# A decoder layer on one core: the end of its mixture-of-experts stage rewritten, and a four-expert pass moved to place 3

## The chip, the cores and the metric

The kernel runs on one core of a Trainium2 chip. The metric is the device time of one execution in microseconds (us). The time before is 546.1 us, the median of three runs (546.03 to 546.58).

## What is computed

One layer of a decoder with 512 tokens of width 1024, all float32: a projection, an mLSTM and a sliding-window attention, a first layer norm, then a hierarchical mixture of experts and a second layer norm. The change touches only the last part:

```python
x = layer_norm(ALPHA * x + y, ln1_w, ln1_b)
# router: top-1 group of 4, then top-2 of its 8 experts, weights in combine[token, expert]
for e in range(32):
    h = silu(x @ w_gate[e]) * (x @ w_up[e])          # 1024 -> 256
    out = out + combine[:, e:e+1] * (h @ w_down[e])  # 256 -> 1024
x = layer_norm(ALPHA * x + out, ln2_w, ln2_b)
```

Each expert has three matrices of 1 MB (gate, up, down), so 96 MB of weights are read once.

## The kernel before

**Passes.** The experts run in 13 passes of 128 seats each. ORDER names the kind of each pass: a B pass has two experts with 64 seats each, an A pass two with 96 and 32, a C pass four with 32 each. Before, ORDER is BBBABABACBBCC, with passes 0 to 12. A B or an A pass reads 6 MB, a C pass 12 MB. A pass takes these steps on TensorE: its tokens' rows are picked by one-hot matmuls (`pairs_x`, line 1005, for two passes at once, in odd passes, for the next two), gate and up (`pass_gu`, line 1092, in four parts; the transposes of the pass before stand ahead of the fourth), then, one pass later, the transposed product of the pass (`dn_t`, lines 1113 and 1115) and its down (`pass_dn`, line 1123).

**Combining.** The down results of passes 0 to 7 are scaled and written to DRAM (`y_store`, line 1141); in passes 8 and 9 `y_gather` fetches them token by token in eight indirect DMAs (line 1149), and VectorE adds them to x1 (line 1152). Later passes are split into a high and a low part (`y_split`, lines 1133 and 1134) and put back on their tokens by one-hot matmuls, with an add on VectorE for each half row (`add_back`, lines 1171 and 1172).

**Weights.** SyncE's queue issues every weight load, in the order of the passes, within a pass gate and up of k 0 to 511 of each expert, then of k 512 to 1023, then down. Each load of 1 MB takes one of 16 slots (`prefetch`, `load_part`); a slot is handed on in the order in which passes release gate and up, and a pass later down. So a load waits until an older pass has used its slot. I number the 96 slots' loads in order; the first 18 are passes 0 to 2.

**The end.** After pass 11 has run its gate and up in the loop, a block with a written order for TensorE, VectorE, ScalarE and GpSimd follows (line 1627 on): a first quarter of pass 12's gate and up (`last_gu`), pass 11's down, `add_back` by chunks of 128 tokens, and between them for each chunk `norm_s` (statistics on VectorE, then three small GpSimd instructions, lines 198, 199 and 1587), `norm_z` (ScalarE line 1595, multiply line 1596), the rest of pass 12's gate and up, `base_rows` (the rows of pass 12's tokens, for its own norm), pass 12's transposes and down, and `norm_o` (add, line 1601, and output DMA). At last pass 12's tokens are normed apart and scattered over the output (line 1697). On each engine the instructions of this block run in the order in which they are written. In the loop only TensorE's order is written.

Of the kernel before, what the change touches and what calls it, by code (L numbers as in the profile page):

```python
# [27 lines left out]
DE = 256  # L28
CAP = 64

ORDER = "BBBABABACBBCC"
NP = len(ORDER)
STATIC = 6
NOVER = 32
# [44 lines left out]
def layer_kernel(ctx, tc, x, w_in, conv_w, conv_b, gate_bias, norm_w, sinks, w_out, ln1_w, ln1_b,  # L79
# [30 lines left out]
    def rslot(name, dt=F32, n=DM):  # L110
        key = free.pop(0)
        return slot(name, dt, key)[:, :n], key
# [476 lines left out]
        return a.rearrange("(p j) n -> p j n", p=P)  # L589


    def load_part(ts, e, i):
        if i < 2:
            t = ts[0].rearrange("p (w j n) -> p w j n", w=2, j=4)
            for w, src in enumerate((w_gate[0], w_up[0])):
                SP.dma_start(t[:, w], rows_of(src, e)[:, 4 * i:4 * i + 4])
            return t
        src = rows_of(w_down[0], e)
        if len(ts) == 1:
            SP.dma_start(ts[0].rearrange("p (j n) -> p j n", j=2), src)  # L600
# [12 lines left out]
    def expert(r):  # L613
        if r < STATIC:
            return r
        if r not in ids:
            ids[r] = SP.value_load(eid[0:1, r:r + 1], min_val=0, max_val=NE - 1)
        return ids[r]

    def release(p, down):  # L620
        free.extend(k for k in KEYS[p][down] if k != "mix")

    def prefetch(n):
        while loads and free and n > 0:
            p, i, b = loads.pop(0)
            if free[0] == "mix":
                key, ts = free.pop(0), [slot("we")[:, :DM] for _ in range(2)]
            else:
                t, key = rslot("we", n=2 * DM)
                ts = [t]  # L630
            assert key != "mix" or i == 2
            KEYS[p][i == 2].append(key)
            pairs[p][b][i] = load_part(ts, expert(SEATS[p][b]), i)
            n -= 1


# [430 lines left out]
    def taken(p, t):  # L1067
        return pairs_g(t) if p in GATHER else pairs_x(t, min(2, NP - p))
# [93 lines left out]
    def toks(p):  # L1162
        return [t[:, p:p + 1] for t in tok2]
# [374 lines left out]

    def l2_fill(i):
        d, w = l2d  # L1540
        t = rslot("l2")[0]
        l2.append(t)
        for u in range(2):
            g = 2 * i + u
            p_ = bank("l2")
            for s in range(2):
                TE.matmul(p_, w[:, g:g + 1].to_broadcast([16, P]), d[:, s].rearrange("p k n -> p (k n)"),
                          start=s == 0, stop=s == 1)
            A.copy(t[:, 512 * u:512 * u + 512], p_)

    with tc.manual_schedule(engines={ENG.PE}):
        for p in range(2, NP - 1):
            release(p, False)
            if p > 2:
                release(p - 1, True)
            prefetch(99)
            hts = []
            pg = pg2 if p == 2 else pass_gu(xs, p % 2, p, (lambda: hts.append(dn_t(prev))) if prev else None)
            if prev:
                ht = hts[0]  # L1560
            h = pair_h(pg)
            if p % 2:
                xs = taken(p + 1, hn)
                if p + 3 < NP:
                    hn = ready(p + 3)
            if prev:
                py = pass_dn(ht, p - 1)
                if p - 1 < KEPT:
                    y_store(py, p - 1)
                else:  # L1570
                    y = y_split(py, cws[:, p - 1:p], *y_slots())
                    add_back(back_hot(slot("oh2", F32R)[:, 0:T], toks(p - 1)), y)
                if p - KEPT in (0, 1):
# [15 lines left out]
    zo = {}  # L1589

    def norm_z(c):
        z = zo[c] = rslot("z")[0]
        mv = mvs[c]
        for h, hs in enumerate(HS):
            A.activation(z[:, hs], x1[c][:, hs], AF.Identity, bias=mv[:, 3:4], scale=mv[:, 2:3])
            (G if ('VV', 'VG', 'VV', 'GV')[c][h] == "G" else V).tensor_mul(z[:, hs], z[:, hs], l2[0][:, hs])
# [11 lines left out]
    def same_rows():
        m, w = rslot("same")[0][:, 0:P], W.tile([P, DE], F32, name="hid", bufs=1)
        tk = tok2[0][:, p:p + 1]  # L1610
        b = bank("same", tag="t")
        TE.matmul(b[:, 0:P], tk.to_broadcast([P, P]), ident, start=True, stop=True)
        V.tensor_scalar(m, b[:, 0:P], tk, None, op0=OP.is_equal)
        V.scalar_tensor_tensor(w[:, 0:P], triu, 0.5, m, op0=OP.is_lt, op1=OP.mult)
        V.tensor_reduce(w[:, P:P + 1], w[:, 0:P], axis=AX.X, op=OP.add)
        V.tensor_scalar(w[:, P + 1:P + 2], tk, 0.0, None, op0=OP.is_lt)
        V.tensor_add(w[:, P:P + 1], w[:, P:P + 1], w[:, P + 1:P + 2])
        V.scalar_tensor_tensor(row[:, 0:1], w[:, P:P + 1], BIG, tk, op0=OP.mult, op1=OP.add)
        return m

    p = NP - 1
    release(p - 1, True)
    prefetch(99)
    l2d = l2_parts()
    o = back_hot(slot("oh2", F32R)[:, 0:T], toks(p - 1))
    with tc.manual_schedule(engines=MAN):
        ob = hots(p, P)
        pg = bank("pg")
        zr = [bank("zr", tag=t) for t in ("t", "m")]
        fin = {}  # L1630

# [12 lines left out]
        def last_gu(u, g):
            gu_part(pg, xs, 0, pairs[p], TILES[ORDER[p]], 2 * u + g)
            if g:
                k = len(SEATS[p])
                free.extend(KEYS[p][0][k * u:k * u + k])

        last_gu(0, 0)  # L1650
        ht = dn_t(prev)
        py = pass_dn(ht, p - 1)
        y = y_split(py, cws[:, p - 1:p], *y_slots())
        add_back(o, y, (0,))
        norm_s(0, base(0))
        l2_fill(0)
        add_back(o, y, (1,))
        l2_fill(1)
        norm_s(1, base(1))
        norm_z(0)  # L1660
        last_gu(0, 1)
        add_back(o, y, (2,))
        x1_fin(0)
        last_gu(1, 0)
        norm_s(2, base(2))
        sm = same_rows()
        add_back(o, y, (3,))
        base_rows(0)
        norm_z(1)
        base_rows(1)  # L1670
        last_gu(1, 1)
        norm_s(3, base(3))
# [12 lines left out]
        A.activation(held_y[:, HS[0]], py[0], AF.Copy, scale=cws[:, p:p + 1])
        A.activation(held_y[:, HS[1]], py[1], AF.Copy, scale=cws[:, p:p + 1])
        release(p, True)
        for h in range(2):
            TE.matmul(zr[h], sm, held_y[:, HS[h]], start=False, stop=True)
        norm_s(4, zr)  # L1690
        mv = mvs[4]
        z = rslot("z")[0]
        for h, hs in enumerate(HS):
            V.scalar_tensor_tensor(z[:, hs], zr[h], mv[:, 0:1], l2[0][:, hs], op0=OP.subtract, op1=OP.mult)
        for h, hs in enumerate(HS):
            V.scalar_tensor_tensor(z[:, hs], z[:, hs], mv[:, 2:3], l2[1][:, hs], op0=OP.mult, op1=OP.add)
        G.indirect_dma_start(out=o2[:, :], out_offset=bass.IndirectOffsetOnAxis(ap=row[:, 0:1], axis=0),  # L1697
                             in_=z, in_offset=None, bounds_check=T - 1, oob_is_err=False)
# [26 lines left out]
    free[:] = ["ring0"] * 4 + ["ring1"] * 2 + ["ring2"] + ["ring0", "ring1", "ring0", "ring2"]  # L1725
# [61 lines left out]
```

## Time and profile before

| what | value |
|---|---|
| median of the runs | 546.1 us |
| the profiled execution | 546.19 us, of which the span of instructions is 544.5 us |
| TensorE busy | 491.1 us (90%) |
| VectorE busy | 286.5 us (53%) |
| bytes read from DRAM | 126.58 MB |
| weights stream, main queue | 62.6% of 16 DMA engines' span |

Shares are averages over stages with different limits. The page also cuts the span into 40 slices of 13.6 us; in it TensorE is full from slice 21 to 28, the DMA engines are full from slice 20 to 36, and neither is full in the last three slices.

### The profile page before, as it was taken

Reading aid. Unit: us, or ns where it says so; the run is one execution under the profiler, and the core shown is the slowest. Engines: PE = TensorE matmul, PEld = TensorE weight load, DVE = VectorE, ACT = ScalarE, POOL = GpSimd, SP = SyncE. Lnnn points to the kernel's source line nnn. Section 1 sums busy time; section 2 is a strip of 40 time slices with the busy share of each in tenths; the row PEclk is TensorE's granted clock in tenths of the full one; section 3 lists DMA queues with packets and bytes.
Section 4 is the critical chain, followed back from the end, with each engine's and each line's share of the span. In section 5 each row is a group of like instructions: output and inputs, shape, how many; then the busy total and the mean of one; then the engine's idle time right before and its main releaser. Section 6 shows DMA issues by size and latency. Waiting matters only on the chain. (4 is left out here: it accounts for less than half of the span.)

```text
span 544.5 us, 8460 instructions
## 1 busy us (share of the span) xinstructions
PE 491.1 (90%) x3048; PEld 336.3 (62%) x3048; DVE 286.5 (53%) x643; ACT 162.6 (30%) x352; POOL 155.7 (29%) x179
## 2 busy tenths in 40 slices
PE   6999799999999999979899999999958687997990
PEld 5999688879889978768736463635413532362430
DVE  3453687874387675687881230210200564426883
ACT  3552555785543511505301112111110011020530
POOL 5479804322201103634900000000113031001451
PEclk9999979999999999987699999999987789998996
DMA  8624212221964637368379999999999999998003
GB/s 231 198 79 125 71 38 77 78 78 43 378 238 117 219 108 228 105 283 315 150 239 417 353 381 343 402 422 381 370 421 421 422 417 421 380 381 348 1 25 150
DMA packets 43885, 134.12 MB, mean 246 GB/s; under 512 B 6673, under 2 KB 17953, under 8 KB 40000
## 3 DMA queue, kind: packets, MB, share of 16 engines
q1 hardware_dynamic: 40928, 126.04, 62.6%
q0 software_dynamic: 2912, 7.50, 3.8%
q8 instruction: 25, 0.41, 0.3%
q14 instruction: 20, 0.16, 0.1%
HBM read 126.58 MB, written 8.91 MB: 249 GB/s over the span
## 5 line engine op out<-in xcount | busy, mean ns | idle before, releaser
L1092 PE MATMUL pg<-we,xs 128*32 128x512 f32 (+1 forms) x608 | 102.0, 606 | 8.7 <-DMA we<-in_w_exp_up 8.7
L1092 PEld LDWEIGHTS pg<-we,xs 128*32 128x32 f32 (+1 forms) x608 | 27.7, 121 | 67.6 <-issue 65.5
L1005 PE MATMUL xp<-ohr,x1h 128*128 128x256 f32 (+1 forms) x224 | 59.7, 304 | 7.1 <-DVE ht L1115 5.3
L244 PE MATMUL pj<-wh,xh 128*128 128x256 f32 (+1 forms) x224 | 63.7, 286 | 1.1 <-ACT wh L189 1.1
L245 PE MATMUL pj<-wh,xl 128*128 128x256 f32 (+1 forms) x224 | 62.8, 282 | 0.4 <-DVE xl L190 0.4
L1005 PE MATMUL xp<-ohr,x1l 128*128 128x256 f32 (+1 forms) x224 | 58.2, 297 | 0.0
L1123 PE MATMUL yo<-we,ht 128*32 128x512 f32 (+1 forms) x304 | 49.2, 620 | 6.5 <-DVE ht L1115 6.5
L1005 PEld LDWEIGHTS xp<-ohr,x1h 128*128 128x128 f32 x224 | 46.6, 208 | 12.9 <-DVE ht L1115 5.5
L249 PE MATMUL pj<-wl,xh 128*128 128x256 f32 x192 | 52.5, 279 | 0.0
L1005 PEld LDWEIGHTS xp<-ohr,x1l 128*128 128x128 f32 x224 | 46.5, 208 | 0.0
L244 PEld LDWEIGHTS pj<-wh,xh 128*128 128x128 f32 x224 | 42.4, 189 | 1.3 <-ACT wh L189 1.3
L245 PEld LDWEIGHTS pj<-wh,xl 128*128 128x128 f32 x224 | 42.4, 189 | 0.7 <-DVE xl L190 0.6
L1105 ACT ACTIVATE hid<-pg 128x256 f32<-128x256 f32 x13 | 5.0, 386 | 117.4 <-PE pg L1092 117.4
L1141 POOL DMA_DIRECT2D yd<-y x8 | 4.4, 552 | 124.5 <-ACT y L1140 124.5
L1123 PEld LDWEIGHTS yo<-we,ht 128*32 128x32 f32 (+1 forms) x304 | 14.5, 123 | 35.2 <-issue 25.4
L249 PEld LDWEIGHTS pj<-wl,xh 128*128 128x128 f32 x192 | 35.6, 188 | 0.0
L1115 DVE COPY ht<-ph 128x256 f32<-128x256 f32 x13 | 5.5, 422 | 55.3 <-PE ph L1113 55.3
L190 DVE TENSOR_TENSOR wl<-wraw,wh 128x1024 fp32r<-128x1024 f32 x14 | 21.4, 1543 | 22.8 <-ACT wh L189 19.1
L189 ACT ACTIVATE wh<-wraw 128x1024 fp32r<-128x1024 f32 (+2 forms) x23 | 23.2, 1023 | 12.4 <-DMA wraw<-in_w_in 3.7
L193 PE MATMUL pj<-xh,wh 128*128 128x512 f32 x64 | 26.5, 414 | 0.0
L195 PE MATMUL pj<-xl,wh 128*128 128x512 f32 x64 | 26.5, 414 | 0.0
L194 PE MATMUL pj<-xh,wl 128*128 128x512 f32 x64 | 26.1, 408 | 0.0
(359 smaller groups left out, 971.3 us busy)
## 6 DMA issues: line engine op xcount, KB each, us to landing
we<-in_w_exp_gate SPq DMA_DIRECT2D x64, 512.0 KB
we<-in_w_exp_up SPq DMA_DIRECT2D x64, 512.0 KB
we<-in_w_exp_down SPq DMA_DIRECT2D x30, 1024.0 KB
wraw<-in_w_in SPq DMA_DIRECT2D x20, 512.0 KB
yd<-y POOLq DMA_DIRECT2D x8, 512.0 KB, 7.7
xc<-in_x SPq DMA_DIRECT2D x4, 512.0 KB
wo<-in_w_out SPq DMA_DIRECT2D x8, 256.0 KB
wo<-in_w_out SPq DMA_DIRECT2D x4, 512.0 KB
```

Of the source, the lines that this page charges most:

```text
L189: A.activation(hi, src, AF.Copy)
L190: eng.tensor_tensor(lo, src, hi, op=OP.subtract)
L193: TE.matmul(o, lh, rh, start=start, stop=False)
L194: TE.matmul(o, ll, rh, start=False, stop=False)
L195: TE.matmul(o, lh, rl, start=False, stop=stop)
L244: TE.matmul(o, xh[j // 2][:, j % 2, cs], ws[i][j][0], start=j == 0, stop=False)
L245: TE.matmul(o, xl[j // 2][:, j % 2, cs], ws[i][j][0], start=False, stop=False)
L249: TE.matmul(o, xh[k // 2][:, k % 2, cs], ws[i][k][1], start=False, stop=k == 7)
L1005: TE.matmul(p_[:, j2, 0:P * n], w[c][:, 2 * g + j2], o[:, c, 0:P * n], start=c == 0 and s == 0 and j2 == 0, stop=c == NCH - 1 and s == 1 a ...
L1092: TE.matmul(pg[s:s + n], xs[k // 4][:, k % 4, P * b + s:P * b + s + n], ws[e][k // 4][:, :, k % 4], start=k == 0, stop=k == 7)
L1115: V.tensor_copy(ht, ph)
L1123: TE.matmul(py[u][s:s + n], ht[:, j, s:s + n], wt[e][2][j][:, 512 * u:512 * u + 512], start=j == 0, stop=j == 1)
```

## The change

ORDER becomes BBBCABABACBBC: one of the last two four-expert passes goes from place 11 to place 3, and the passes between move one place back. The down weights of pass 12 are loaded in two halves, first the half j=0 of its four experts, then the half j=1. In the last pass of the loop (p = 11) the transposes of pass 11 stand ahead of the `add_back` of pass 10. The one-hot rows of pass 12 (`ob`) are the tile made for its pick in the loop and are not built a second time, and `same_rows` moves into the loop's block. In the end block all of pass 12's gate and up stands behind pass 11's `add_back`, in two halves; its second half stands behind the norms of all four chunks. Some tiles come from the mix pool and no longer from the weights' slots. One of two scalings of pass 12's result moves from ScalarE to VectorE. The core of the diff:

```diff
-ORDER = "BBBABABACBBCC"
+ORDER = "BBBCABABACBBC"
...
+    loads.extend((NP - 1, 3, b) for b in range(len(SEATS[-1])))
...
+            last = p == NP - 1 and i == 2
+            if last:
+                late[b] = ts[0]
+            pairs[p][b][i] = load_part(ts, expert(SEATS[p][b]), i, 0 if last else None)
...
             if p % 2:
-                xs = taken(p + 1, hn)
+                ob, xs = hn, taken(p + 1, hn)
...
                     y = y_split(py, cws[:, p - 1:p], *y_slots())
+                    if p == NP - 2:
+                        ht = dn_t(h)
-                    add_back(back_hot(slot("oh2", F32R)[:, 0:T], toks(p - 1)), y)
+                    add_back(back(p - 1), y)
...
+        l2d = l2_parts()
+        o = back(NP - 2)
+        sm = same_rows(NP - 1)
...
-        ob = hots(p, P)
...
-        last_gu(0, 0)
-        ht = dn_t(prev)
-        py = pass_dn(ht, p - 1)
-        y = y_split(py, cws[:, p - 1:p], *y_slots())
+        y = y_split(pass_dn(ht, p - 1), cws[:, p - 1:p], *y_slots())
         add_back(o, y, (0,))
-        norm_s(0, base(0))
         l2_fill(0)
         add_back(o, y, (1,))
         l2_fill(1)
+        norm_s(0, base(0))
+        x1_fin(0)
+        add_back(o, y, (2,))
+        norm_z(0)
+        add_back(o, y, (3,))
+        pg = bank("pg")
+        last_gu(0)
         norm_s(1, base(1))
-        norm_z(0)
-        last_gu(0, 1)
-        add_back(o, y, (2,))
-        x1_fin(0)
-        last_gu(1, 0)
+        norm_o(0)
+        norm_z(1)
+        base_rows(0)
         norm_s(2, base(2))
-        sm = same_rows()
-        add_back(o, y, (3,))
-        base_rows(0)
-        norm_z(1)
         base_rows(1)
-        last_gu(1, 1)
+        norm_o(1)
+        norm_z(2)
+        base_rows(2)
         norm_s(3, base(3))
+        base_rows(3)
+        norm_o(2)
+        norm_z(3)
+        last_gu(1)
         h = pair_h(pg)
-        norm_z(2)
-        norm_z(3)
-        base_rows(2)
         ht = dn_t(h)
-        norm_o(0)
-        base_rows(3)
-        norm_o(1)
-        norm_o(2)
         norm_o(3)
         py = pass_dn(ht, p)
...
-        A.activation(held_y[:, HS[1]], py[1], AF.Copy, scale=cws[:, p:p + 1])
+        V.tensor_scalar(held_y[:, HS[1]], py[1], cws[:, p:p + 1], None, op0=OP.mult)
```

## Rows read from the trace of the kernel before

**Rows 1.** The page: DMA share and GB/s, 40 slices.
```profile
DMA  8624212221964637368379999999999999998003
GB/s 231 198 79 125 71 38 77 78 78 43 378 238 117 219 108 228 105 283 315 150 239 417 353 381 343 402 422 381 370 421 421 422 417 421 380 381 348 1 25 150
```

**Rows 2.** Timeline of SyncE's queue: start, duration; the last weight loads.
```profile
484.49 4.56 SPq L600 DMA_DIRECT2D we<-in_w_exp_down  x4
```

**Rows 3.** Timeline of TensorE, passes 8 and 9: start, duration, idle before.
```profile
393.78 1.88 PE L1092 MATMUL pg<-we,xs 128*32 128x512 f32 x10 [1.10 <-DMA we<-in_w_exp_up]
...
407.18 1.94 PE L1092 MATMUL pg<-we,xs 128*64 128x512 f32 x2 [5.81 <-DMA we<-in_w_exp_up]
...
418.82 1.94 PE L1092 MATMUL pg<-we,xs 128*64 128x512 f32 x8
...
428.14 0.58 PE L1005 MATMUL xp<-ohr,x1h 128*128 128x256 f32 x1 [5.31 <-DVE ht L1115]
```

**Rows 4.** Stretches: busy time by engine, then TensorE's clock, DMA share, GB/s.
```profile
312.00:316.00 4.00, 4.00 (x38) 1.25 (x34) 0.42 (x1) 0.00 (x0) 0.00 (x0) 1.00 0.92 295
...
328.00:332.00 4.00, 4.00 (x22) 1.41 (x20) 0.00 (x0) 1.13 (x2) 0.53 (x1) 1.00 0.74 247
332.00:336.00 4.00, 4.00 (x22) 1.14 (x22) 0.42 (x1) 0.00 (x0) 0.00 (x0) 1.00 1.01 343
```

**Rows 5.** Timelines of GpSimd and VectorE: the gathers of pass 8 and behind them.
```profile
410.73 1.12 POOL L1149 DMA_INDIRECT yg<-yd,yrow  x1 [5.89 <-issue]
...
426.53 1.23 DVE L1152 TENSOR_TENSOR x<-x,yg 128x1024 f32<-128x1024 f32 x1 [0.67 <-DMA yg<-yd,yrow]
427.67 0.42 DVE L1115 COPY ht<-ph 128x256 f32<-128x256 f32 x1
```

**Rows 6.** Timeline of TensorE, from pass 11's gate and up to its down.
```profile
468.83 5.36 PE L1092 MATMUL pg<-we,xs 128*32 128x512 f32 x48
...
487.29 1.05 PE L1092 MATMUL pg<-we,xs 128*32 128x512 f32 x4
...
494.78 1.90 PE L1092 MATMUL pg<-we,xs 128*32 128x512 f32 x10
...
499.87 5.34 PE L1123 MATMUL yo<-we,ht 128*32 128x512 f32 x32 [2.75 <-DVE ht L1115]
```

**Rows 7.** Timeline of VectorE, from pass 11's result to pass 12's down.
```profile
505.14 1.61 DVE L1134 SCALAR_TENSOR_TENSOR yl<-yo,cws,yh 128x512 fp32r<-128x512 f32 x2 [5.32 <-ACT yh L1133]
506.66 1.37 DVE L1172 TENSOR_TENSOR x<-x,cb 128x512 f32<-128x512 f32 x2
507.94 1.28 DVE L1583 BATCH_NORM_STATS2 lnst<-x 128x6 f32<-128x512 f32 x2
...
512.05 1.40 DVE L1596 TENSOR_TENSOR z<-z,l 128x512 f32<-128x512 f32 x2
...
525.76 0.41 DVE L1115 COPY ht<-ph 128x256 f32<-128x256 f32 x1
526.10 5.53 DVE L1601 TENSOR_TENSOR z<-z,l 128x512 f32<-128x512 f32 x6
```

**Rows 8.** Timeline of GpSimd: first and last small instruction of two chunks' norms.
```profile
509.56 0.24 POOL L198 TENSOR_SCALAR lnmv<-lnmv 128x1 f32<-128x1 f32 x1 [12.30 <-DVE lnmv L1585]
...
510.56 0.27 POOL L1587 TENSOR_SCALAR lnmv<-lnmv 128x1 f32<-128x1 f32 x1
512.14 0.69 POOL L198 TENSOR_SCALAR lnmv<-lnmv 128x1 f32<-128x1 f32 x1 [1.31 <-DVE lnmv L1585]
...
513.98 0.27 POOL L1587 TENSOR_SCALAR lnmv<-lnmv 128x1 f32<-128x1 f32 x1
```

**Rows 9.** Timeline of ScalarE: chunk 1's two halves in norm_z.
```profile
514.28 1.52 ACT L1595 ACTIVATE z<-x,lnmv 128x512 f32<-128x512 f32 x2 [0.61 <-POOL lnmv L1587]
```

**Rows 10.** Timeline of TensorE: the downs of passes 9 and 12.
```profile
458.35 3.65 PE L1123 MATMUL yo<-we,ht 128*64 128x512 f32 x16 [2.73 <-DVE ht L1115]
...
526.23 3.64 PE L1123 MATMUL yo<-we,ht 128*32 128x512 f32 x32 [1.02 <-DVE ht L1115]
```

More of the change, by code (lines that the diff above doesn't have):

```diff
@@ L589, in rows_of, with load_part @@
         return a.rearrange("(p j) n -> p j n", p=P)
-    def load_part(ts, e, i):
+    def load_part(ts, e, i, js=None):
         if i < 2:
@@ L599, in load_part @@
         if len(ts) == 1:
-            SP.dma_start(ts[0].rearrange("p (j n) -> p j n", j=2), src)
+            t = ts[0].rearrange("p (j n) -> p j n", j=2)
+            if js is None:
+                SP.dma_start(t, src)
+            else:
+                SP.dma_start(t[:, js], src[:, js])
             return [ts[0][:, 0:DM], ts[0][:, DM:2 * DM]]
@@ L621, in release @@
         free.extend(k for k in KEYS[p][down] if k != "mix")
+    loads.extend((NP - 1, 3, b) for b in range(len(SEATS[-1])))
+    late = {}
     def prefetch(n):
-        while loads and free and n > 0:
+        while loads and (free or loads[0][1] == 3) and n > 0:
             p, i, b = loads.pop(0)
+            if i == 3:
+                load_part([late[b]], expert(SEATS[p][b]), 2, 1)
+                continue
             if free[0] == "mix":
@@ L632, in prefetch @@
             KEYS[p][i == 2].append(key)
-            pairs[p][b][i] = load_part(ts, expert(SEATS[p][b]), i)
+            last = p == NP - 1 and i == 2
+            if last:
+                late[b] = ts[0]
+            pairs[p][b][i] = load_part(ts, expert(SEATS[p][b]), i, 0 if last else None)
             n -= 1
@@ L1540, in l2_fill @@
         d, w = l2d
-        t = rslot("l2")[0]
+        t = slot("l2")[:, :DM]
         l2.append(t)
@@ L1549, in l2_fill, with same_rows, back @@
             A.copy(t[:, 512 * u:512 * u + 512], p_)
+    def same_rows(p):
+        t = slot("same")
+        m, w = t[:, 0:P], t[:, P:2 * P + 2]
+        tk = tok2[0][:, p:p + 1]
+        b = bank("same", tag="t")
+        TE.matmul(b[:, 0:P], tk.to_broadcast([P, P]), ident, start=True, stop=True)
+        V.tensor_scalar(m, b[:, 0:P], tk, None, op0=OP.is_equal)
+        V.scalar_tensor_tensor(w[:, 0:P], triu, 0.5, m, op0=OP.is_lt, op1=OP.mult)
+        V.tensor_reduce(w[:, P:P + 1], w[:, 0:P], axis=AX.X, op=OP.add)
+        V.tensor_scalar(w[:, P + 1:P + 2], tk, 0.0, None, op0=OP.is_lt)
+        V.tensor_add(w[:, P:P + 1], w[:, P:P + 1], w[:, P + 1:P + 2])
+        V.scalar_tensor_tensor(row[:, 0:1], w[:, P:P + 1], BIG, tk, op0=OP.mult, op1=OP.add)
+        return m
+    def back(p):
+        return back_hot(slot("oh2", F32R)[:, 0:T], toks(p))
     with tc.manual_schedule(engines={ENG.PE}):
@@ L1558, in layer_kernel @@
             pg = pg2 if p == 2 else pass_gu(xs, p % 2, p, (lambda: hts.append(dn_t(prev))) if prev else None)
-            if prev:
-                ht = hts[0]
             h = pair_h(pg)
             if p % 2:
-                xs = taken(p + 1, hn)
+                ob, xs = hn, taken(p + 1, hn)
                 if p + 3 < NP:
@@ L1566, in layer_kernel @@
             if prev:
-                py = pass_dn(ht, p - 1)
+                py = pass_dn(hts[0], p - 1)
                 if p - 1 < KEPT:
@@ L1591, in norm_z @@
     def norm_z(c):
-        z = zo[c] = rslot("z")[0]
+        z = zo[c] = slot("z")[:, :DM]
         mv = mvs[c]
@@ L1605, in base @@
         return [x1[c][:, hs] for hs in HS]
[L1608 to L1619, printed above, removed]
     p = NP - 1
@@ L1623, in layer_kernel @@
     prefetch(99)
-    l2d = l2_parts()
-    o = back_hot(slot("oh2", F32R)[:, 0:T], toks(p - 1))
     with tc.manual_schedule(engines=MAN):
-        ob = hots(p, P)
-        pg = bank("pg")
         zr = [bank("zr", tag=t) for t in ("t", "m")]
@@ L1642, in base_rows, with last_gu @@
                     TE.matmul(zr[h], ob[:, c, 0:P].bitcast(F32), x1[c][:, HS[h]], start=c == 0, stop=False)
[L1644 to L1648, printed above, removed]
-        last_gu(0, 0)
-        ht = dn_t(prev)
-        py = pass_dn(ht, p - 1)
-        y = y_split(py, cws[:, p - 1:p], *y_slots())
+        def last_gu(u):
+            for g in range(2):
+                gu_part(pg, xs, 0, pairs[p], TILES[ORDER[p]], 2 * u + g)
+        y = y_split(pass_dn(ht, p - 1), cws[:, p - 1:p], *y_slots())
         add_back(o, y, (0,))
-        norm_s(0, base(0))
         l2_fill(0)
@@ L1658, in layer_kernel @@
         l2_fill(1)
-        norm_s(1, base(1))
-        norm_z(0)
-        last_gu(0, 1)
-        add_back(o, y, (2,))
-        x1_fin(0)
-        last_gu(1, 0)
+        norm_s(0, base(0))
[5 more added lines that the diff above has]
+        last_gu(0)
+        norm_s(1, base(1))
+        norm_o(0)
+        norm_z(1)
+        base_rows(0)
         norm_s(2, base(2))
-        sm = same_rows()
-        add_back(o, y, (3,))
-        base_rows(0)
-        norm_z(1)
         base_rows(1)
-        last_gu(1, 1)
+        norm_o(1)
+        norm_z(2)
+        base_rows(2)
         norm_s(3, base(3))
+        base_rows(3)
+        norm_o(2)
+        norm_z(3)
+        last_gu(1)
         h = pair_h(pg)
-        norm_z(2)
-        norm_z(3)
-        base_rows(2)
         ht = dn_t(h)
-        norm_o(0)
-        base_rows(3)
-        norm_o(1)
-        norm_o(2)
         norm_o(3)
         py = pass_dn(ht, p)
-        held_y = rslot("yf")[0]
+        held_y = slot("yf")[:, :DM]
         A.activation(held_y[:, HS[0]], py[0], AF.Copy, scale=cws[:, p:p + 1])
-        A.activation(held_y[:, HS[1]], py[1], AF.Copy, scale=cws[:, p:p + 1])
-        release(p, True)
+        V.tensor_scalar(held_y[:, HS[1]], py[1], cws[:, p:p + 1], None, op0=OP.mult)
         for h in range(2):
@@ L1691, in layer_kernel @@
         mv = mvs[4]
-        z = rslot("z")[0]
+        z = slot("z")[:, :DM]
         for h, hs in enumerate(HS):
@@ L1723, in dyn_pair @@
         add_back(back_hot(slot("oh2", F32R)[:, 0:T], [tk[:, i:i + 1] for i in range(2)]), y)
-    free[:] = ["ring0"] * 4 + ["ring1"] * 2 + ["ring2"] + ["ring0", "ring1", "ring0", "ring2"]
+    free[:] = ["ring0"] * 4 + ["ring1"] * 2 + ["ring2"]
     nmore = nc.values_load(more[0:1, 1:2], min_val=0, max_val=1)
```

## Prediction, made before the changed kernel was run

> **What bounds the kernel now.** I read the page's slices first, then the timelines backwards from the end. The slices show the weights streaming at about 420 GB/s until slice 36, then nothing [rows 1]. The last four downs are issued at 484.5 to 489 [rows 2] and slice 36 ends at 503.6, so every weight is in the chip by about 502; pass 12's down starts only at 526.23 [rows 10]. The last 42 us of the span are therefore not waiting for weights, and splitting the last down into halves can by itself save nothing: its cover is the 24 us between those two numbers, and it costs something only if the compute ahead of it came 24 us earlier.
>
> Going back from pass 12's down: its transposed tile is copied by VectorE at 525.76, and VectorE has been nearly full since pass 11's result came at 505.14 [rows 7]. Pass 11's down stood 2.75 us idle for VectorE, which was building one-hot rows, and then took 5.34 us [rows 6], where a down at full clock takes 3.65 [rows 10]. Before that, TensorE runs pass 11's gate and up from 468.83 [rows 6]. What sets 468.83 is further back: pass 9's gate and up waited 5.81 us for its first weights, and the pick behind it waited 5.31 us for VectorE [rows 3], which stood in its queue behind the adds of gathered rows [rows 5]. From there to 468.83 TensorE runs its passes one behind the other. So three points carry the end: when pass 9 is over, what lies between 468.83 (I call it S) and 505.14 (call it R, pass 11's result on VectorE), and VectorE's list from R to pass 12's down (D, 526.23).
>
> **Part 1: place 3, up to S.** Weights come in one order at one rate. Pass 9's gate and up is over when its last weights are in: before, that is load 64 (18 for passes 0 to 2, 30 for A B A B A, 12 for the C, 4 more); after, load 68, for pass 9 is then the C with eight gate and up loads. Load 61 landed at 407.18 [rows 3]. At 421 GB/s [rows 1] a load of 1.049 MB takes 2.49 us, so seven more take 17.4 us; a store and four gathers among them, some 1.3 MB, another 3.1 us: load 68 would land at 427.7 at the pace of before. The four-expert pass at place 3 has eight slots to release in one gate and up instead of four, so the stream doesn't thin where it does now: at 295, 247 and 343 GB/s for 4 us each against 421, that is 1.2 + 1.65 + 0.75 = 3.6 us [rows 4]. Load 68 then lands at 424.1, and the rest of the gate and up behind it (3 of 8 k steps at half clock, the transposes) ends near 428.6. Before, it ended at 420.76, but the pick had 1.9 us of work done and started again at 428.14 [rows 3], as if it had been free from 426.2. So S moves by 428.6 - 426.2 = **+2.4 us**.
>
> Bounds. If the stream gives back more than those three windows, pass 9 waits for nothing more than the gathers, and these come earlier by the 1.10 us and a like wait in pass 8's gate and up that go: -2.1. If pass 7 has to wait for weights too, later is the other end: load 56 landed at 393.78 [rows 3], load 52 four loads before it at the 2.68 us that lie between loads 56 and 61, less 3.6, at 379.5, while pass 7's gate and up would want it near 373. Then downs 6 and 7, the last store and the gathers behind it come 4.9 us later, and the copy at 427.67 that frees the pick stands behind them [rows 5]: +4.9. I take +2.4, because the landing at 407.18 is measured on the same stream and the gathers' place in VectorE's queue is not yet known. Passes 10 to 12 need fewer loads after that than before, and have them in time.
>
> **Part 2: from S to R.** Before, 36.3 us (468.83 to 505.14). Gone: the one-hot rows (2.75 us of idle TensorE), one quarter of gate and up ahead of the down (1.8), the slow down (5.34 - 3.65 = 1.7) [rows 6]. Transposes (0.5) move ahead into a gap. Added ahead of the down: the matmul of `same_rows` (0.5) and a copy of 0.4 in VectorE's queue; its five other instructions run under the down. Together -5.8. More is possible: the matmuls at 487.29 belong to the end block, yet run in the gaps of pass 10's `add_back` [rows 6]; if pass 11's down slips in likewise, VectorE's own list from 487.3 (split 1.5, one-hot rows 1.3, eight adds 5.1 [rows 7], copy 0.4, `same_rows` 1.3 and 0.3 more: 9.9 us) sets R at 497.2, which is -7.9. I take the middle, **-6.7**, since only part of a quarter slipped in before.
>
> **Part 3: from R to D.** Before, 21.1 us. VectorE runs this block in its written order. Its list before hid: split 1.61, four adds of 1.28, four statistics of 1.5, four multiplies by chunk (1.4 for two halves, 0.7 where GpSimd has one), `same_rows` 1.5, hid and the copy 0.4 each: about 19.6, and 1.5 us of waiting. After, `same_rows` is gone but `norm_o` of chunks 0, 1 and 2 (1.4, 1.4 and 0.7) moves from behind the copy [rows 7] to ahead of hid: 21.7 us of work and 0.6 of transposes. The new order puts only one short step (an add or an output add, 0.7 to 1.4 us) between a chunk's statistics and its multiply. Between them lie three GpSimd instructions, 1.27 us from first start to last end [rows 8], 0.1 of hand-over, and ScalarE's half, 0.76, the second half 0.76 later [rows 9]: 2.2 us to the first half and 3.0 to the second. VectorE then stands 1.0, 0.9, 0.9 and 2.3 us for chunks 0 to 3, and the last stands ahead of hid on ScalarE and on VectorE. With the first add's start this gives hid at R + 26.6 and D at R + 28.2: +7.1. In the second chunk the GpSimd steps took 2.11 us instead of 1.27 (512.14 to 514.25, the first one 0.69 instead of 0.24) while VectorE multiplied z by l [rows 7, 8]; after, output adds of that same kind run under two or more of the chunks' steps, 0.85 each: +8.8 or +9.1. I take **+8.8**. TensorE is done earlier (about R + 22.8: four adds' matmuls 5.7, two fills 2.4, gate and up 7.5, base rows 6.7), so VectorE decides.
>
> The Trainium skill ("SBUF — State Buffer", section "Who interferes with whom") says that a VectorE instruction with two SBUF inputs contends with a GpSimd instruction that reads SBUF and that the loser blocks entirely. The 0.69 and 2.11 us agree in direction; by the rule all four chunks would be hit when an output add starts first, which as an estimate would be a further 1.7 us and 553.6 in all; by the rows two are, and the sum goes by these.
>
> **Part 4: the clock.** TensorE waits 4 to 6 us for hid. After 2.73 us of waiting pass 9's down ran at full pace, 3.65 [rows 10]; after 2.75 pass 11's took 5.34 [rows 6]; after 5.31 the picks' first matmuls took 0.58 [rows 3]. The coming wait is nearest to the third: **+1.7**, bounds 0 and 2.1.
>
> **Part 5: from D to the end.** Before, 18.3 us. VectorE's six output adds (to 531.6, [rows 7]) no longer stand ahead of the last statistics, and one scaling is on an idle engine: **-0.5** (0.3 to 0.8). The three outputs leave earlier; only the fourth is near the scatter. The eight half loads are issued while the queue is full of loads, so they cost nothing that a later step sees.
>
> **Sum.** 2.4 - 6.7 + 8.8 + 1.7 - 0.5 = +5.7. The profiled execution took 546.19 us (span 544.5 and 1.7 around it), 0.1 above the median of its runs: 546.2 + 5.7 = 551.9 us.
>
> **Rivals.** (a) *The gathers late*: part 1 at +4.9 and part 3 at +9.1: 554.7 us. For it: the stream is full from slice 28 on [rows 1] and load 52 falls behind. Against: a wait of pass 7 also shortens later waits. (b) *The end is as long as it was*: the down slips into the gaps (-7.9), GpSimd isn't slowed (+7.1), half of the clock's loss (+0.8), S as before: 546.2 - 7.9 + 7.1 + 0.8 - 0.5 = 545.7, and up to 549 with S at +2.4. (c) *Faster*: the round over GpSimd and ScalarE costs VectorE no wait, because the steps of the next chunk cover it; then part 3 is only the work that moved, +1.2, TensorE doesn't idle and the clock holds: 546.2 + 2.4 - 6.7 + 1.2 - 0.5 = 542.6. It decides at the point where one intervening VectorE step is as long as 2.2 us; rows 7 show 1.4, which speaks against it; for it speaks that the three GpSimd steps alone, 1.27, are hidden by it. That the last down in halves is what counts can be left aside: it would need weights that are late, and they are 24 us early.
>
> **Chances.** The forecast (549 to 554) 0.45; (a) 0.13; (b) 0.18, of which 0.10 lies within 0.2% of the time before; (c) 0.24. A measurement of this kernel can tell about 0.2%, 1.1 us, from no change. Slower 0.45 + 0.13 + 0.08 = 0.66, same 0.10, faster 0.24. The range, 542.3 to 557, takes in (c), (a) and the upper bounds of the clock and of the slowed GpSimd; the forecast's own cases lie in 549 to 554.
>
> **What would show it.** Right: pass 9's gate and up waits 10 us or more for weights and S lies at 470 to 472; pass 11's down takes 3.65 us without a wait; VectorE idles ahead of line 1596's multiplies for ScalarE four times; TensorE idles some 4 us ahead of the last transposes; no weight lands after R. Wrong: S well before 468, R to D under 24 us, or weights that arrive after the last gate and up wants them, which would make the halves matter.

## The result, and the profile after

The changed kernel took 562.9 us (median of 4 runs, 558.6 to 566.5) against 546.1 us before: a ratio of 1.031, 95% interval 1.022 to 1.040. It is slower, as forecast, but by three times as much: 16.9 us and not 5.7. Its profiled execution took 565.51 us (span 563.8), 2.6 us above its median, so the sums below, made on profiles, come to +19.3 us of span and not to 16.9.

| stretch | before, us | after, us | change | forecast |
|---|---|---|---|---|
| start to pass 11's gate and up (S) | 468.8 | 481.6 | +12.8 | +2.4 |
| S to pass 11's result on VectorE (R) | 36.3 | 30.4 | -5.9 | -6.7 |
| R to pass 12's down (D) | 21.1 | 32.2 | +11.1 | +8.8 |
| D to the end | 18.3 | 19.5 | +1.2 | +1.7 - 0.5 |

The first row is counted from the start of the span. In the changed kernel's trace pass 0's gate and up starts at 268.29 and not at 269.78 (among all profiles here it lies between 265.8 and 269.8, whatever the edit), so counted from there S moved by 14.3 us.

The page of the changed kernel, its DMA share and GB/s in 40 slices of 14.1 us, is the answer to [rows 1]:

```profile
DMA  8644203214935562965599999999999999950110
GB/s 238 177 113 113 76 2 111 76 40 140 415 99 168 188 175 99 341 235 245 180 372 380 370 409 391 415 412 402 402 421 420 420 421 357 347 183 0 75 76 19
```

The stream thins less in slices 20 to 28 than it did, and it is over in slice 35, by 507.4 us; pass 12's down starts at 544.29. As before, the end doesn't wait for weights.

The loss ahead of S shows in TensorE's timeline (start, duration, idle before and what ended it): a wait of pass 7's gate and up, the last waits of pass 9's, the pick behind it, pass 9's down, and S. Line 1106 is line 1092 of before, 1019 is 1005, 1137 is 1123 and 1129 is 1115; it answers [rows 3] and the first of [rows 10]:

```profile
377.33 2.53 PE L1106 MATMUL pg<-we,xs 128*64 128x512 f32 x6 [2.58 <-DMA we<-in_w_exp_up]
...
418.76 1.02 PE L1106 MATMUL pg<-we,xs 128*32 128x512 f32 x2 [1.42 <-DMA we<-in_w_exp_up]
421.97 2.74 PE L1106 MATMUL pg<-we,xs 128*32 128x512 f32 x10 [2.19 <-DMA we<-in_w_exp_up]
...
425.27 2.38 PE L1106 MATMUL pg<-we,xs 128*32 128x512 f32 x16
427.58 0.38 PE L1019 MATMUL xp<-ohr,x1h 128*128 128x256 f32 x1
...
435.44 0.58 PE L1019 MATMUL xp<-ohr,x1h 128*128 128x256 f32 x1 [5.72 <-DVE ht L1129]
...
468.39 6.42 PE L1137 MATMUL yo<-we,ht 128*32 128x512 f32 x32 [6.85 <-DVE ht L1129]
...
481.64 2.80 PE L1106 MATMUL pg<-we,xs 128*64 128x512 f32 x12
```

The two copies (`ht`) that TensorE waits for stand in VectorE's queue behind adds of gathered rows. VectorE's timeline, the answer to [rows 5]:

```profile
423.86 1.23 DVE L1166 TENSOR_TENSOR x<-x,yg 128x1024 f32<-128x1024 f32 x1 [21.07 <-DMA yg<-yd,yrow]
...
430.61 1.23 DVE L1166 TENSOR_TENSOR x<-x,yg 128x1024 f32<-128x1024 f32 x1 [2.23 <-DMA yg<-yd,yrow]
433.83 1.23 DVE L1166 TENSOR_TENSOR x<-x,yg 128x1024 f32<-128x1024 f32 x1 [1.99 <-DMA yg<-yd,yrow]
434.97 0.42 DVE L1129 COPY ht<-ph 128x256 f32<-128x256 f32 x1
...
463.72 1.23 DVE L1166 TENSOR_TENSOR x<-x,yg 128x1024 f32<-128x1024 f32 x1 [6.60 <-DMA yg<-yd,yrow]
466.78 1.23 DVE L1166 TENSOR_TENSOR x<-x,yg 128x1024 f32<-128x1024 f32 x1 [1.83 <-DMA yg<-yd,yrow]
467.92 0.42 DVE L1129 COPY ht<-ph 128x256 f32<-128x256 f32 x1
```

So the last weights of pass 9 were in and its matmuls done at 427.6; the pick then ran 16 matmuls and stopped for a copy of pass 8's product, which stood behind the fourth add. GpSimd's timeline has the last store and the gathers that follow it. The last of the first four gathers was issued at 419.51 and added 14.3 us later:

```profile
406.50 0.53 POOL L1155 DMA_DIRECT2D yd<-y  x1 [8.61 <-DMA we<-in_w_exp_up]
...
415.47 1.12 POOL L1163 DMA_INDIRECT yg<-yd,yrow  x1 [6.59 <-issue]
...
419.51 0.99 POOL L1163 DMA_INDIRECT yg<-yd,yrow  x1 [0.30 <-issue]
```

In the kernel before, the same two instructions stand as follows, and the add of [rows 5] came 11.8 us behind the second:

```profile
402.45 0.53 POOL L1141 DMA_DIRECT2D yd<-y  x1 [10.74 <-ACT y L1140]
...
414.77 0.99 POOL L1149 DMA_INDIRECT yg<-yd,yrow  x1 [0.30 <-issue]
```

From R on, VectorE's timeline answers to [rows 7] (line 1631 is 1596, 1630 is 1595, 1636 is 1601):

```profile
516.70 0.69 DVE L1186 TENSOR_TENSOR x<-x,cb 128x512 f32<-128x512 f32 x1 [1.70 <-PE cb L1185]
...
520.71 0.69 DVE L1186 TENSOR_TENSOR x<-x,cb 128x512 f32<-128x512 f32 x1 [1.03 <-PE cb L1185]
...
522.17 2.54 DVE L1631 TENSOR_TENSOR z<-z,l 128x512 f32<-128x512 f32 x2
...
530.17 0.69 DVE L1631 TENSOR_TENSOR z<-z,l 128x512 f32<-128x512 f32 x1 [1.68 <-ACT z L1630]
...
535.20 1.40 DVE L1631 TENSOR_TENSOR z<-z,l 128x512 f32<-128x512 f32 x2 [1.67 <-ACT z L1630]
...
541.28 1.40 DVE L1631 TENSOR_TENSOR z<-z,l 128x512 f32<-128x512 f32 x1 [2.68 <-ACT z L1630]
```

TensorE waits at the end of it for the last product (`hid`) and then runs the down slowly, at a granted clock of 0.50 from 544 to 548:

```profile
543.07 0.70 PE L1127 MATMUL ph<-ident,hid 128*128 128x128 f32 x2 [5.26 <-DVE hid L1120]
544.29 6.02 PE L1137 MATMUL yo<-we,ht 128*32 128x512 f32 x32 [0.52 <-DVE ht L1129]
```

### The profile page after: what moved, and what is told of

It is laid out like the page before. It is cut to its first block, busy times and chain, and to the rows that moved or that the text cites. A ratio compares the mean times of both kernels' runs of the same rounds, so it can differ in the third digit from the quotient of the medians.

```text
span 563.8 us, 8436 instructions
## 1 busy us (share of the span) xinstructions
PE 501.7 (89%) x3048; PEld 337.6 (60%) x3048; DVE 282.8 (50%) x635; ACT 162.2 (29%) x351; POOL 154.8 (27%) x179
## 5 line engine op out<-in xcount | busy, mean ns | idle before, releaser
L1106 PE MATMUL pg<-we,xs 128*32 128x512 f32 (+1 forms) x608 | 105.5, 611 | 11.5 <-DMA we<-in_w_exp_up 11.4
L1019 PE MATMUL xp<-ohr,x1h 128*128 128x256 f32 (+1 forms) x224 | 58.4, 299 | 7.5 <-DVE ht L1129 5.7
L1137 PE MATMUL yo<-we,ht 128*32 128x512 f32 (+1 forms) x304 | 54.1, 671 | 8.0 <-DVE ht L1129 8.0
L1019 PE MATMUL xp<-ohr,x1l 128*128 128x256 f32 (+1 forms) x224 | 56.9, 293 | 0.0
L1166 DVE TENSOR_TENSOR x<-x,yg 128x1024 f32<-128x1024 f32 x8 | 9.8, 1224 | 35.8 <-DMA yg<-yd,yrow 35.8
```

Of the source, the lines that this page charges most:

```text
L1019: TE.matmul(p_[:, j2, 0:P * n], w[c][:, 2 * g + j2], o[:, c, 0:P * n], start=c == 0 and s == 0 and j2 == 0, stop=c == NCH - 1 and s == 1 a ...
L1106: TE.matmul(pg[s:s + n], xs[k // 4][:, k % 4, P * b + s:P * b + s + n], ws[e][k // 4][:, :, k % 4], start=k == 0, stop=k == 7)
L1137: TE.matmul(py[u][s:s + n], ht[:, j, s:s + n], wt[e][2][j][:, 512 * u:512 * u + 512], start=j == 0, stop=j == 1)
L1166: V.tensor_add(x1[c], x1[c], t)
```

## The experiments

Kernels that were sent together ran on one chip and share its runs of the kernel before (medians 546.3, 544.7 and 544.3 us in three groups). The ratio on record, with its interval, isn't always the quotient of the two medians (e2: 1.011 against 1.007); where they differ I name both. Then come the landmarks of each profiled execution, in us, "to R" counted from the first matmul of pass 0's gate and up. One execution is profiled of each kernel, and executions differ by some us:

| kernel | median us | ratio to before (95%) | to R | R to D | D to end |
|---|---|---|---|---|---|
| before | 546.1 | | 235.4 | 21.1 | 18.3 |
| after | 562.9 | 1.031 (1.022 to 1.040) | 243.8 | 32.2 | 19.5 |
| e1, order alone | 556.7 | 1.023 (1.013 to 1.033) | 241.7 | 21.3 | 19.4 |
| e2, end alone | 550.3 | 1.011 (1.006 to 1.015) | 228.8 | 33.1 | 18.5 |
| e3, after, gather adds on GpSimd | 550.9 | 1.008 (1.004 to 1.013) | 232.4 | 31.6 | 18.6 |
| e4, before, gather adds on GpSimd | 537.9 | 0.989 (0.979 to 0.999) | 225.3 | 23.1 | 18.2 |
| e5, after, end block interleaved as before | 558.1 | 1.028 (1.021 to 1.034) | 241.4 | 27.1 | 18.6 |
| e6, e5 with old order and gather adds on GpSimd | 531.6 | 0.976 (0.968 to 0.984) | 222.0 | 27.1 | 18.7 |
| e7, e5 with gather adds on GpSimd | 542.4 | 0.994 (0.989 to 1.000) | 228.6 | 27.0 | 18.6 |
| e8, after, each `norm_z` a chunk later | 557.6 | | 241.5 | 27.7 | 17.0 |
| e9, e6 with a quarter of gate and up in the gap | 533.2 | 0.980 (0.974 to 0.986) | 218.3 | 22.7 | 19.5 |
| e10, after, last down in one piece | 560.6 | 1.028 (1.023 to 1.034) | 239.2 | 33.2 | 18.3 |

**Which half of the change loses.** e1 is the kernel before with the new order only, e2 the changed kernel with the old order.

```diff
-ORDER = "BBBABABACBBCC"
+ORDER = "BBBCABABACBBC"
```

> The kernel before with only the order of the changed one (the four-expert pass at place 3); the end block stays as it was. Theory A (place 3 moves the start S of pass 11's gate and up by +12.8 us, because pass 8's and 9's transposed copies stand behind the gathers' adds in VectorE's queue and the gathers come later): S near 481, and 546.1 + 12.8 = 559 us, the stretches from S to R, from R to D and from D on as in the kernel before (36.3, 21.1, 18.3). Theory B (the late S comes out of the rewritten end's other use of buffers, and place 3 costs the +2.4 us of the forecast): 548.5 us.

```diff
-ORDER = "BBBCABABACBBC"
+ORDER = "BBBABABACBBCC"
```

> The changed kernel with the old order of passes. If the end is what it was in the changed kernel (S to R 30.4, R to D 32.2, D to the end 19.5 us) and S is back at 468.8, the sum is 546.1 - 5.9 + 11.1 + 1.2 = 552.5 us. Rival: the long stretch from R to D in the changed kernel came from the late S and the slow clock behind it, and the rewritten end saves what its shorter S to R says: 540 to 546 us.

e1 measured 556.7 us, 10.3 above before on its chip (2.3% by the ratio, some 12); e2 550.3, 4.0 above (1.1%, some 6), which is not the 540 to 546 of its rival. Both halves lose, and their sum, 14.3 by the medians and some 18 by the ratios, lies about the 16.9 of the whole. The order's loss lies ahead of R (R to D is 21.3, as before), the end's behind it: up to R the new end is 6.5 us faster than before, and from R to D 12.0 slower. The profile of e1 is of the fastest of its runs (550.7), with S at 471.8 where theory A had 481; in it the pick waited only 0.5 us and the down behind it 5.2. So its landmark of 241.7 understates the median's.

**The adds of gathered rows.** In the changed kernel (e3) and in the one before (e4) these adds go to GpSimd, which issues the gathers, and so out of VectorE's queue.

```diff
-                V.tensor_add(x1[c], x1[c], t)
+                G.tensor_add(x1[c], x1[c], t)
```

> The changed kernel with the eight adds of gathered rows (line 1166) on GpSimd instead of VectorE. Theory A (these adds hold the copies that free TensorE): the waits of 5.72 us in the pick and 6.85 us ahead of pass 9's down go, and so does the slow clock in that down (2.8), S comes near 468, 549 to 552 us. Rival (weights are next: passes 9 to 11 wait for their loads anyway): S stays above 477, at most 4 us gained, 559 us or more.

> The kernel before with the same eight adds on GpSimd. Theory A: the waits of 5.31 and 2.73 us go, 538 us. Rival (pass 10 or 11 then waits for weights, or add_back waits for GpSimd's slower adds): 543 to 547 us.

e3 measured 550.9, e4 537.9 us, both as theory A had it. In e3's timeline of TensorE the pick and pass 9's down start without a wait:

```profile
429.81 0.39 PE L1019 MATMUL xp<-ohr,x1h 128*128 128x256 f32 x1
...
457.28 3.64 PE L1137 MATMUL yo<-we,ht 128*32 128x512 f32 x32
```

and the gathers come hardly earlier, as its timeline of GpSimd has it:

```profile
434.76 2.41 POOL L1166 TENSOR_TENSOR x<-x,yg 128x1024 f32<-128x1024 f32 x1 [1.33 <-DMA yg<-yd,yrow]
```

The fourth add starts 0.9 us later than in the changed kernel (counted from pass 0's gate and up, 0.5 us earlier) and takes twice as long, and no copy stands behind it. So the two waits, 5.72 and 6.85 us, were an effect of the queue.

The move has a price of its own. While GpSimd adds, VectorE's one-hot steps take longer: two of them 4.59 us, where two like ones took 0.61 in the changed kernel, and one 2.49 instead of 0.34. Behind the latter TensorE's `add_back` waited 2.42 us. From e3's timeline of VectorE:

```profile
434.52 4.59 DVE L1012 TENSOR_SCALAR ohr<-iot,pcol 128x256 fp32r<-128x256 f32 x2
...
462.55 2.49 DVE L1173 TENSOR_SCALAR oh<-iot,tok 128x256 fp32r<-128x256 f32 x1
```

And e4 shows that the kernel before paid for the like waits: it gains 8.5 us of median by the same edit (by the ratio 1.1%, some 6, and hardly clear of nothing), the changed kernel about 12 (562.9 to 550.9, though these two ran on different chips). The waits alone are therefore only some 4 to 6 us of what the change added, and place 3 must cost more by itself.

**What place 3 costs without the gather waits.** e6 and e7 have the adds on GpSimd and an end block interleaved as before (e5's); they differ in ORDER alone.

> The kernel before with three things: gathers' adds on GpSimd, and from the change the early down of pass 11 with reused one-hot rows (S to R) and its other edits, with the old interleave behind it; old order of passes. If the parts add: 537.9 (adds on GpSimd) - 7 (S to R 30.4 instead of 37.4) = 531 us. Rival: with TensorE this early the last passes wait for weights (the stream ends near 500 in every run), and the parts don't add: 535 us or more.

> As the run with the old order, new front and GpSimd adds, but with the four-expert pass at place 3. Theory A: without the gathers' adds in the way, place 3 costs what four more loads ahead of pass 9's end cost: S some 3 us behind the kernel before and 10 to 14 behind the same kernel with the old order, 541 to 544 us. Rival: place 3 costs nothing any more and both orders give the same time within 2 us.

e6 measured 531.6 us, e7 542.4, in runs of one chip, as their theories had it (531; 541 to 544): place 3 costs 10.8 us with no gather in VectorE's way. TensorE's groups from pass 0's gate and up to R (line, shapes, count | busy us, mean ns | idle before, and for what) show where. e6:

```profile
L1106 PE MATMUL pg<-we,xs 128*64 128x512 f32 x224 | 55.5, 628 | 7.8 <-DMA we<-in_w_exp_up 7.8
...
L1106 PE MATMUL pg<-we,xs 128*32 128x512 f32 x320 | 37.4, 595 | 0.1
```

e7:

```profile
L1106 PE MATMUL pg<-we,xs 128*64 128x512 f32 x224 | 54.7, 611 | 2.6 <-DMA we<-in_w_exp_up 2.5
L1106 PE MATMUL pg<-we,xs 128*32 128x512 f32 x320 | 45.0, 628 | 9.3 <-DMA we<-in_w_exp_up 9.3
```

The same number of matmuls, busy and waiting together: 100.8 us in e6, 111.6 in e7. Of these 10.8 us, 4.0 are waits for weights (now in the four-expert pass, which takes its loads one by one), and 6.8 are busy time, in the short pieces between those waits: in e7 two matmuls by themselves are busy 1.02 us at 403.22, where 48 in one piece are 5.33, and the granted clock falls to 0.50 in the last stretch of waits (420 to 424). All that while the stream runs at 418 to 425 GB/s, so TensorE goes at its pace. Four more loads ahead of pass 9's end at 2.49 us each are, as an estimate, 10.0 us; no run tests that reading by itself. For the changed kernel and e2 the same rows give 109.0 and 100.4, +8.6; TensorE's waits for `ht` are 13.1 against 8.2, +4.9; and the downs are 1.4 longer: together 14.9, the whole difference of their R (243.8 - 228.8 = 15.0).

```profile
L1106 PE MATMUL pg<-we,xs 128*64 128x512 f32 x224 | 54.5, 608 | 3.7 <-DMA we<-in_w_exp_up 3.7
L1106 PE MATMUL pg<-we,xs 128*32 128x512 f32 x320 | 42.9, 604 | 7.9 <-DMA we<-in_w_exp_up 7.7
...
L1137 PE MATMUL yo<-we,ht 128*32 128x512 f32 x160 | 21.0, 671 | 6.8 <-DVE ht L1129 6.8
```

These are the changed kernel's. (The two profiles e6 and e7 differ by 6.5 in R and not by 10.8, since e6's is of its slowest run, in which the matmuls of `add_back` and their waits took 5.5 us more. In it a GpSimd add again held a one-hot step of VectorE, for 2.00 us instead of 0.34. That the 10.8 of these rows equals the 10.8 of the medians is therefore in part chance.)

**The order of the end block.** e5 keeps the new front (transposes ahead, `same_rows` and one-hot rows early) and puts the steps behind pass 11's down back into the order of before.

```diff
         add_back(o, y, (0,))
+        norm_s(0, base(0))
         l2_fill(0)
...
-        norm_s(0, base(0))
-        x1_fin(0)
-        add_back(o, y, (2,))
+        norm_s(1, base(1))
         norm_z(0)
+        add_back(o, y, (2,))
+        x1_fin(0)
...
         last_gu(0)
+        norm_s(2, base(2))
+        add_back(o, y, (3,))
...
```

> The changed kernel, but in the end block, behind pass 11's down, the steps stand in the order of the kernel before (each chunk's multiply two or more VectorE steps behind its statistics, all output adds behind the transposed copy); the order of passes, the early down, the reused one-hot rows stay. Theory A (the written order of norm steps costs the 11.1 us between R and D): R to D 20 to 23 us, TensorE's slow clock in the last down gone, about 551 us. Rival (TensorE's own list, one quarter of gate and up longer than before, is what makes it long): R to D 27 us or more, 557 us or more.

R to D fell to 27.1, half way, and the time is 558.1: both lie where the rival had them (27 or more, 557 or more). So the written order costs 5 us from R to D, and 6 us more than before remain. Part of what remains is TensorE's clock, and stretches of 4 us show it. Those of the changed kernel (busy time of PE, PEld, DVE, ACT, POOL, then TensorE's granted clock, DMA share, GB/s):

```profile
512.00:516.00 4.00, 3.00 (x8) 1.64 (x9) 3.00 (x8) 1.03 (x2) 0.00 (x0) 0.88 0.00 0
516.00:520.00 4.00, 4.00 (x9) 2.31 (x8) 2.78 (x5) 1.16 (x3) 0.22 (x1) 0.50 0.00 0
520.00:524.00 4.00, 4.00 (x12) 1.86 (x14) 3.12 (x3) 2.60 (x4) 3.23 (x4) 0.50 0.00 0
```

and of e5:

```profile
512.00:516.00 4.00, 4.00 (x10) 2.24 (x11) 3.49 (x8) 1.17 (x2) 1.08 (x3) 0.64 0.00 0
516.00:520.00 4.00, 4.00 (x12) 2.13 (x15) 2.75 (x6) 2.86 (x5) 1.06 (x3) 0.50 0.00 0
520.00:524.00 4.00, 4.00 (x24) 0.91 (x20) 3.05 (x6) 2.09 (x3) 3.06 (x3) 0.58 0.00 0
```

0.50 is 1.2 GHz. In the kernel before:

```profile
500.00:504.00 4.00, 4.00 (x24) 1.01 (x24) 0.00 (x0) 0.00 (x0) 0.00 (x0) 0.59 0.28 117
...
516.00:520.00 4.00, 4.00 (x20) 2.15 (x22) 3.77 (x11) 0.00 (x0) 2.99 (x5) 1.00 0.02 4
```

Before, the clock was low in pass 11's down, which ran in one piece up to its split, TensorE waited only 0.28 us for that, and the clock was 0.99 to 1.00 from 504 to 524. In both kernels here the down is over early, in the gaps of pass 10's `add_back`; TensorE has nothing to run while VectorE works towards the split (it waits 1.29 and 1.28 us for it and is busy 3.00 of 4 us, in e5 2.42 from 508 to 512). Then the clock goes down, and the matmuls of `add_back` are late for VectorE (1.70 and 1.03 us above).

**The quarter put back.** e9 takes e6 and puts the first quarter of pass 12's gate and up between pass 11's down and its split (and one scaling back on ScalarE).

```diff
-        y = y_split(pass_dn(ht, p - 1), cws[:, p - 1:p], *y_slots())
+        py = pass_dn(ht, p - 1)
+        pg = bank("pg")
+        gu_part(pg, xs, 0, pairs[p], TILES[ORDER[p]], 0)
+        y = y_split(py, cws[:, p - 1:p], *y_slots())
...
-        last_gu(0)
+        gu_part(pg, xs, 0, pairs[p], TILES[ORDER[p]], 1)
```

> The run with old order, new front and GpSimd adds, with two edits: a first quarter of pass 12's gate and up stands between pass 11's down and its add_back, so that TensorE has work while pass 11's result is split, and the second scaling of pass 12's result is on ScalarE again. Theory (TensorE's slow clock behind the 1.3 us without matmuls lengthens R to D, and the scaling on VectorE waits 1.3 us behind the output adds): R to D 26.6 becomes 22 to 24, D to the end 18.7 becomes about 17.5, 526 to 529 us. Rival (the clock falls anyway, for TensorE runs thin from pass 10's add_back on): R to D stays at 26 and only the 1.3 us of the scaling go, 530 us or more.

The stretches of e6 are, from 488 on:

```profile
488.00:492.00 4.00, 2.59 (x8) 1.41 (x7) 3.97 (x12) 0.39 (x1) 0.00 (x0) 0.87 1.03 421
492.00:496.00 4.00, 4.00 (x10) 2.31 (x8) 3.10 (x7) 1.17 (x3) 1.08 (x3) 0.50 0.70 288
496.00:500.00 4.00, 4.00 (x14) 1.56 (x16) 2.75 (x6) 3.73 (x6) 1.55 (x4) 0.50 0.05 22
```

and of e9:

```profile
488.00:492.00 4.00, 3.96 (x15) 2.26 (x15) 3.97 (x10) 1.08 (x2) 0.42 (x2) 1.00 1.03 421
492.00:496.00 4.00, 4.00 (x15) 1.52 (x17) 3.96 (x8) 3.43 (x5) 2.40 (x5) 0.59 1.01 414
496.00:500.00 4.00, 3.91 (x22) 2.06 (x15) 3.90 (x8) 1.52 (x2) 3.73 (x6) 0.99 0.41 169
```

With the gap filled (3.96 busy of 4 us where e6 has 2.59), the clock is low for one stretch and not for two, and R to D is 22.7 and not 27.1: the mechanism shows in the trace, though some of the quarter's own 1.9 us now lies ahead of R. It isn't the whole of it: the clock still falls to 0.59 in e9, and to 0.62 for one stretch in e4, which has the quarter in place too, so what makes it fall isn't settled. The gain of 4 us doesn't show in the time: 533.2 against 531.6, which is where the rival had it (530 or more). With e6's runs from 528.1 to 536.0 and e9's from 530.8 to 535.5, what the quarter is worth in time can't be told.

**The round over GpSimd and ScalarE.** e8 puts each `norm_z` of the changed kernel one chunk later, so that the next chunk's statistics cover the round.

```diff
         add_back(o, y, (2,))
+        norm_s(1, base(1))
         norm_z(0)
...
-        norm_s(1, base(1))
-        norm_o(0)
+        norm_s(2, base(2))
         norm_z(1)
+        norm_o(0)
...
```

> The changed kernel with each norm_z and norm_o one chunk's statistics later in the written order; the same VectorE work stands ahead of hid. Theory A (waits for the round over GpSimd and ScalarE are most of the 11.1 us): the waits of 1.7, 1.7 and 2.7 us ahead of the multiplies shrink below 1, R to D near 27, 556 to 558 us. Rival (the output adds ahead of hid and the slow clock carry it): R to D stays at 30 or more, 561 us or more.

R to D is 27.7, 4.5 less than in the changed kernel, and the time 557.6 (549.7 to 560.1, against 544.7 before on its chip; no interval), as theory A had it. Of the three waits only the last remains, and one of 1.22 us for ScalarE ahead of `hid` is new. VectorE's timeline of e8:

```profile
534.19 1.45 DVE L1631 TENSOR_TENSOR z<-z,l 128x512 f32<-128x512 f32 x1 [1.64 <-ACT z L1630]
```

**The last down's halves.** e10 loads pass 12's down in one piece, as before.

> The changed kernel with pass 12's down weights loaded in one piece for each expert, as before. Theory: the last weights are in the chip 40 us ahead of the last down, so the halves neither help nor cost: 558 to 567 us, R to D 31 to 33. Rival: the eight smaller transfers lengthen the stream or hold SyncE's output DMAs: 3 us or more faster, 555 us or less.

560.6 us: the halves neither help nor harm by more than can be told here, as the weights are in the chip long before.

## Why the prediction was right and wrong

**What bounds the kernel** held: no weight lands behind R, the halves of the last down do nothing that can be told (e10), and VectorE's list from R to D, with its waits, sets the end.

**Part 1 failed.** It said +2.4, and S came 12.8 later. The stream itself was forecast well: pass 9's gate and up ended at 427.65, against 428.6 in the forecast and 420.76 before. The step that failed is the one behind it, "as if it had been free from 426.2": it let 5.4 of the 7.8 us by which pass 9 was to be late hide in the wait for the gathers, and held the gathers where they were. None of it was hidden. The rows of gate and up show 8.6 us more than with the old order, the waits for `ht` 4.9 more on top, and with the adds out of VectorE's way place 3 still cost 10.8 (e6, e7). (From pass 0's gate and up, S stands at 201.9 in e3, only 2.9 behind the unchanged kernel's 199.0; but that one has the gather waits, and e4, the same kernel without them, has 188.0.)

The gathers could not hide the lateness because they hang on the stream too. Pass 7 did wait for weights (its gate and up ran from 369.75 to 383.07), which was the case of the upper bound. The store of pass 7 went out at 406.50 instead of 402.45, 4.1 us later where that bound had 4.9. The four gathers followed 4.7 us later than before, and the last then took 14.3 us to be added instead of 11.8, which no bound had. The pick resumed at 435.44 instead of 428.14: 4.7 and 2.5 make the +7.3.

The second four gathers were not priced at all. Two were issued at 455.76 and 457.06, and now both their adds stood ahead of pass 9's `ht` copy in VectorE's queue, where before one did: the down waited 6.85 us instead of 2.73 and started at 468.39, 32.95 us behind the pick instead of 30.21: +2.7. The clock went to 0.50 during that wait (464 to 472), and the down took 6.42 instead of 3.65: +2.8. From there to S the two kernels run alike. 7.3 + 2.7 + 2.8 = 12.8.

**Part 2**: -5.9 against -6.7, next to the first of its two sums (-5.8). Pass 11's down did slip into the gaps of pass 10's `add_back`, in pieces from 501.24 to 509.58, but it stretched these gaps: a chunk took 2.14 us, where a chunk of pass 9's took 1.51 without such a piece. Filling another's gaps was counted as free and wasn't.

**Part 3**: right in kind, mis-sized by 2.3 us. VectorE stood three times ahead of `norm_z`'s multiplies, 1.68, 1.67 and 2.68 us, where 1.0, 0.9, 0.9 and 2.3 and two rounds slowed by 0.85 had been put; e8 shows that these waits are the order's and can be covered. GpSimd's first step took 0.55 in chunks 1 to 3 and 0.24 in chunk 0, and the three steps 1.86, 1.86 and 1.57 us where chunk 0's took 1.27: three rounds were slowed, by 1.5 us together, where two had been put at 1.7. In chunk 3, GpSimd's step and VectorE's output add are these:

```profile
538.12 0.55 POOL L198 TENSOR_SCALAR lnmv<-lnmv 128x1 f32<-128x1 f32 x1 [3.80 <-DVE lnmv L1620]
537.96 0.64 DVE L1636 TENSOR_TENSOR z<-z,l 128x512 f32<-128x512 f32 x1
```

The Trainium skill ("SBUF — State Buffer", "Who interferes with whom") would have the step blocked while a VectorE instruction with two SBUF inputs that came first runs. The trace agrees: all three chunks with an output add in front were hit, and in chunk 3 the step ended 0.07 us behind the add (538.67 against 538.60).

Missing from the sum were the waits for `add_back` at half clock (1.70 and 1.03) and chunk 0's multiplies, 2.54 instead of 1.40 while GpSimd ran line 190 for 2.37 us. The forecast's first wait, 1.0, was swallowed by them. The step "TensorE is done earlier" took its durations from rows at full clock; but with the quarter moved away and the down slipped ahead, TensorE stood idle in front of them, and then the clock fell; no price was put on that. e9, which gives a quarter back, has 4.4 us less from R to D than e6.

**Parts 4 and 5**: +1.2 together, as forecast, but by luck: two misses cancel. TensorE waited 5.26 us for `hid` (4 to 6 were said) and the down took 6.02, 2.4 more than before and just past the bound of 2.1; so the rest of the end was 1.1 us shorter, where 0.5 had been put.

**Rivals.** (a) named the right place, gathers that come late, and priced it at 4.9 us from one gate; there were two, the gathers also took longer, and a slow down stood behind the second. (b) and (c) needed an R to D of 28.2 or 22.3; it was 32.2. Of the signs that were named, S at 470 to 472 failed plainly (481.6), and pass 9's gate and up waited 7.7 us for weights, where 10 or more were said.

A version that beats both kernels came out of it: e6, which keeps the old order, the new front and the old interleave of the end, and adds the gathered rows on GpSimd: 531.6 us, a ratio of 0.976 (0.968 to 0.984).

## What to carry to other kernels

A wait that hides another delay can only be counted as cover if it doesn't itself hang on what is delayed: follow its releaser back (here add, gather, store, pass 7's weights) before taking the later of two times. Work that only waits for a transfer belongs in a queue in which nothing stands behind it, even on an engine that takes twice as long; then look at what it slows beside it (here VectorE's one-hot steps). And before moving a piece of matmul work, look whether it bridges a gap: the rows around it were measured at the clock that they had with it in place.

## What the runs showed of the hardware

- A gather of 128 rows issued while the stream runs at about 420 GB/s landed 6.9 to 14.2 us later in the changed kernel (median 9.0); the last scatter, with no stream beside it, took 3.3 us.
- The same add of 128x1024 took 1.22 to 1.23 us on VectorE and 2.35 to 2.41 on GpSimd (e3).
- TensorE's granted clock stood at 0.50 from 516 to 524 us while the engine was recorded busy all of the time, and at 1.00 in the same stage before; what preceded it was 3.00 busy of 4 us from 512 to 516.
- VectorE's two-input multiplies went from 1.40 to 2.54 us for two beside a GpSimd add of 2.37 us, and in e3 a one-hot step of VectorE from 0.34 to 2.49 us beside a GpSimd add of 2.35.
- Executions of one kernel lay further apart than the 0.2% that the prediction took as the measurement's grain: the kernel before ran from 540.1 to 551.6 us in 19 runs on one chip. Why wasn't settled.
